# A two-layer block with product-key experts on one core: pacing the gathered tokens through the expert phase

## The chip, the cores and the metric

One core of a Trainium2 chip runs the whole program. The metric is device time in microseconds (us) of one execution.

## The reference

The input x has 256 tokens of 2048 floats. A first block (a norm, a short gated convolution beside block attention, output projection) and the mixing part of a second block (a convolution branch and a state-space branch, gated) come first. The change lies in what follows, the product-key experts:

```python
def peer(h, w_q, sub_keys, u_tab, v_tab):
    def block(xb):                                   # 128 tokens
        q = (xb @ w_q).reshape(128, 8, 2, 128)
        s = jnp.einsum('thcd,hcnd->thcn', q, sub_keys)
        s_top, i_top = lax.top_k(s, 16)              # 16 of 128 keys, twice per head
        cand = s_top[:, :, 0, :, None] + s_top[:, :, 1, None, :]
        cand_idx = i_top[:, :, 0, :, None] * 128 + i_top[:, :, 1, None, :]
        ...
        best, pos = lax.top_k(cand, 16)
        expert = jnp.take_along_axis(cand_idx, pos, axis=-1)
        gates = jax.nn.softmax(best, axis=-1)
        act = jax.nn.gelu(jnp.einsum('td,thkd->thk', xb, u_tab[expert]))
        return jnp.einsum('thk,thkd->td', gates * act, v_tab[expert])
```

Each token picks 8 x 16 = 128 of 16,384 experts; u_tab and v_tab have a row of 2048 floats for each. The result is added to x, and a last norm gives the output. All is float32.

## The kernel before

**Two ways through the experts.** The last 160 tokens (NT) are done densely: both tables, 128 MB each, pass through SBUF in 128 tiles of 1 MB each, every tile is multiplied by all 160 tokens, and a gate matrix that is zero for experts not chosen weighs the activations in between. The first 96 tokens (NS_) are done by gathering: for three groups of 32 tokens the chosen rows are fetched by indirect DMA, 128 rows (1 MB) at a time, four slots of each of 32 tokens. That is 32 gathers of u and 32 of v for a group, 192 in all, called items here.

**The dense stream.** SyncE loads tiles in a fixed order into a ring of five buffers (`w_load`, line 161). `u_step(i)` makes 16 products of u tile i (line 1458), evacuated with a gelu by ScalarE (line 1461); `v_step(i)` makes 16 products of v tile i (line 1475) into sums that stay in PSUM. First come NU0 = 60 u tiles, then v and u tiles in turn for 136 tiles until the u tiles are used up, then v tiles alone. Before v tile i, VectorE multiplies its activations by gates (`weigh`, line 1323), two tiles ahead in program order. The gates come in 16 blocks, built earlier (`gbuild`), stored to DRAM (`gd`) and loaded back eight rows at a time (`gload`, line 1318). The last LAST v tiles are multiplied bank by bank, and each bank is joined with the residual (line 1546), transposed, squared and multiplied by the last gain (lines 1553 to 1556).

**The gathered stream.** `sparse` handles an item as follows. For u, VectorE multiplies the gathered rows by the token's row and sums them (line 1362); after four of them ScalarE makes the gelu (line 1366). For v, after a multiplication by gates (line 1370), VectorE adds the weighted rows to a sum (lines 1372 and 1374). The v items of four slots come after the u items of the next four. There are five buffers; the gather into a buffer (line 1346) is issued by GpSimd when the item that used it is done. After the third group the four partial sums and the residual's rows are loaded (lines 1386, 1387), added (line 1391), normalised and stored (line 1402). `finish(sp_gen)` puts what is left of this in front of the last bank-by-bank part.

**Who decides the order.** All engines execute in program order. Each step of the dense stream calls `Weave.run(budget)`, which draws work from generators until their stated costs (in ns, the numbers they yield) have used the budget; `None` ends a generator's turn. In `gens` are the top-k of the keys (`topk`), then `sparse`, so that `sparse` gets what the top-k leaves; `fine` holds `gbuild`, run four times inside a step. The budget is 3,000 in the query steps, then 4,200 per u tile, or 1,500 while `gbuild` runs (with 675 x 4 for it), then 1,900 per tile. Budgets set an order of instructions only; an engine that waits for nothing runs ahead of the others. `hand_out` gives the first 128 tokens' indices and gates to `rbuf`, from where the gathers read them, once the top-k of these tokens is complete.

When the last u tile is done GpSimd also loads the residual of the dense tokens into the buffers of the normalised input (line 1510 and after).

Of the kernel before, what the change touches and what calls it, by code (L numbers as in the profile page):

```python
# [26 lines left out]
SG = 3  # L27
NS_ = 32 * SG
# [16 lines left out]
class Weave:  # L45
# [34 lines left out]

    def run_fine(self, budget):
# [17 lines left out]
    def finish(self, gen):  # L99
        for _ in gen:  # L100
            pass
        for q in (self.gens, self.free, self.fine):
            if gen in q:
                q.remove(gen)
# [3 lines left out]
def body(ctx, tc, xT, par, wst, kst, bblk, cblk, gfin, uexp, vexp, out):  # L108
# [126 lines left out]

# [874 lines left out]
    gd = drp.tile([NT // 16, P, P, 16], F32, name="gd")  # L1110
    for c in range(2):
        nc.gpsimd.dma_start(xd2[c], x_s[c])
# [87 lines left out]
    sp_ready = [False]  # L1200

    def hand_out():


        V = nc.vector
        V.scalar_tensor_tensor(out=flat(ab[:, 0]), in0=flat(idx[:, 0]), scalar=float(P), in1=flat(idx[:, 1]),
                               op0=ALU.mult, op1=ALU.add)
        V.tensor_copy(flat(abu[:, 0]), flat(ab[:, 0]))
        V.tensor_copy(abr[:, P:2 * P], flat(gat))
        both = abr.rearrange("p (c s) -> p c s", c=2)  # L1210
        for g in range(SG):
            for q in range(4):
                nc.gpsimd.dma_start(
                    rbuf[32 * q:32 * q + 32, 64 * g:64 * g + 64].rearrange("p (c s) -> p c s", c=2),
                    both[32 * g:32 * g + 32, :, 32 * q:32 * q + 32])
        sp_ready[0] = True

    def topk():
        V = nc.vector
        for tt in range(2):  # L1220
# [21 lines left out]
            V.tensor_copy(ixf, ix)  # L1242
            V.tensor_scalar(abu[:, 0], pos, 4, None, op0=ALU.logical_shift_right)
            V.tensor_scalar(abu[:, 1], pos, 15, None, op0=ALU.bitwise_and)
            V.tensor_copy(ab, abu)
# [5 lines left out]
            yield 2500  # L1251
            o4 = scor[tt].rearrange("p (h a b) -> p h a b", h=8, a=16)
            for c in range(2):
                for h in range(0, NH, 4):
                    for q in range(4):
                        V.tensor_tensor(out=o4[:, h + q], in0=ab[:, c, h + q, :, None].to_broadcast([P, 16, 16]),
                                        in1=iota[:, None, 0:16].to_broadcast([P, 16, 16]), op=ALU.is_equal)
                    for q in range(4):
                        V.tensor_tensor(out=o4[:, h + q], in0=o4[:, h + q],
                                        in1=ixf[:, h + q, c, None, :].to_broadcast([P, 16, 16]), op=ALU.mult)  # L1260
                    V.tensor_reduce(out=idx[:, c, h:h + 4, :], in_=o4[:, h:h + 4], axis=AX.X, op=ALU.add)
                    yield 3900
            if tt == 0:
                hand_out()
# [15 lines left out]
    pend_g = []  # L1280

    def gbuild():
        for t4 in range(NT // 4):
            sg = stg[(t4 // 4) % 2].rearrange("p (i t) -> p t i", t=16)
            pb = GB[t4 % 2]
            t = NS_ + t4 * 4
            nc.vector.tensor_tensor(
                out=S[22][:, (t % 8) * P:(t % 8 + 4) * P].rearrange("p (t j) -> p t j", t=4),
                in0=iota[:, None, :].to_broadcast([P, 4, P]),
                in1=i2T[:, t:t + 4, None].to_broadcast([P, 4, P]), op=ALU.is_equal)  # L1290
            for q in range(4):
                o, tq = oh[1][(t + q) % 8], slice(t + q, t + q + 1)
                if q < 1:
                    nc.scalar.activation(o, iota, AF.Abs, scale=-1.0, bias=i1T[:, tq])
                    nc.scalar.activation(o, o, AF.Relu, scale=ngT[:, tq], bias=gT[:, tq])
                else:
                    nc.vector.tensor_scalar(o, iota, i1T[:, tq], gT[:, tq], op0=ALU.is_equal, op1=ALU.mult)
            yield 1650 - 256 * 1
            pend_g.append((t4, pb, sg))
            if len(pend_g) > 1:  # L1300
                gmm(*pend_g.pop(0))
        while pend_g:
            gmm(*pend_g.pop(0))
            yield 500

    def gmm(t4, pb, sg):
# [5 lines left out]
        if t4 % 4 == 3:  # L1312
            nc.scalar.dma_start(gd[t4 // 4], stg[(t4 // 4) % 2].rearrange("p (i t) -> p i t", t=16))

    gblk = lambda b: stg[b % 2][:, 0:8 * NT].rearrange("p (n i t) -> p n i t", n=NT // 16, i=8)

    def gload(b):
        nc.gpsimd.dma_start(gblk(b), gd[:, :, 8 * b:8 * b + 8, :].rearrange("n p i t -> p n i t"))

    def weigh(i):  # L1320

        a3 = act_at(i).rearrange("p (n t) -> p n t", n=NT // 16)
        nc.vector.tensor_tensor(out=a3, in0=a3, in1=gblk(i // 8)[:, :, i % 8, :], op=ALU.mult)  # L1323
        if i % 8 == 7 and i // 8 + 2 < 16:
            gload(i // 8 + 2)


    acc_s, x_rep, gaddr = S[10], S[19], rbuf.bitcast(U32)
    dots = sqsum

    def sparse():
        V = nc.vector
        while not (sp_ready[0] and ws["n"] >= WU):
            yield None
        gb = slots([5, 6, 7, 12, 13])
        flat_b = [(g, n) for g in range(SG) for n in range(8)]
        items = []
        for j, (g, n) in enumerate(flat_b):
            items += [("u", g, 4 * n + k) for k in range(4)]
            if j:  # L1340
                items += [("v", flat_b[j - 1][0], 4 * flat_b[j - 1][1] + k) for k in range(4)]
        items += [("v", SG - 1, 28 + k) for k in range(4)]

        def gather(m):
            kind, g, k = items[m]
            nc.gpsimd.indirect_dma_start(  # L1346
                out=gb[m % len(gb)][:], out_offset=None, in_=uexp if kind == "u" else vexp,
                in_offset=bass.IndirectOffsetOnAxis(ap=gaddr[:, 64 * g + k:64 * g + k + 1], axis=0))

        def rows(g):  # L1350
            for q in range(4):
                nc.gpsimd.dma_start(x_rep[32 * q:32 * q + 32, :], S[18][32 * g:32 * g + 32, :])

        rows(0)
        for m in range(len(gb)):
            gather(m)
        yield None
        for m, (kind, g, k) in enumerate(items):
            buf = gb[m % len(gb)]
            d, a = dots[:, 32 * g + k:32 * g + k + 1], dots[:, P + 32 * g + k:P + 32 * g + k + 1]  # L1360
            if kind == "u":
                V.tensor_tensor_reduce(out=buf, in0=buf, in1=x_rep, scale=1.0, scalar=0.0,  # L1362
                                       op0=ALU.mult, op1=ALU.add, accum_out=d)
# [3 lines left out]
            else:  # L1367
                if k % 4 == 0:
                    a4 = dots[:, P + 32 * g + k:P + 32 * g + k + 4]
                    V.tensor_tensor(out=a4, in0=a4, in1=rbuf[:, 64 * g + 32 + k:64 * g + 36 + k], op=ALU.mult)  # L1370
                if k == 0:
                    V.tensor_scalar(acc_s, buf, a, None, op0=ALU.mult)
                else:
                    V.scalar_tensor_tensor(out=acc_s, in0=buf, scalar=a, in1=acc_s, op0=ALU.mult, op1=ALU.add)  # L1374
            if m + len(gb) < len(items):
                gather(m + len(gb))
            if kind == "u" and k == 31 and g < SG - 1:
                rows(g + 1)
            if kind == "v" and k == 31:
                for q in range(4):  # L1380
                    nc.gpsimd.dma_start(sd[q, 32 * g:32 * g + 32, :], acc_s[32 * q:32 * q + 32, :])
# [39 lines left out]
    weave.add(sp_gen)  # L1421
# [63 lines left out]
    for i in range(NU0):  # L1485
# [13 lines left out]
    LAST = 4  # L1499
    PACE = 1900.0  # L1500
    n_weighed = 0
    for i in range(P - LAST):
# [16 lines left out]
        v_step(i, PACE)  # L1519
        if NU0 + i < P:  # L1520
            u_step(NU0 + i, PACE)
# [124 lines left out]
```

## Time and profile before

| | |
|---|---|
| median of 3 runs | 2566.34 us (2561.63 to 2566.97) |
| the profiled execution | 2564.76 us, its span 2563.0 us |
| TensorE matmuls, weight loads | 2397.4 us (94%), 2270.2 us (89%) |
| VectorE, ScalarE, GpSimd | 1587.9 (62%), 696.5 (27%), 659.5 us (26%) |
| moved by DMA | 741.94 MB, of it 241.81 MB by GpSimd's queue |

Engine names in profile rows: PE is TensorE, PEld its weight loads, DVE VectorE, ACT ScalarE, POOL GpSimd, SP SyncE. L1458 is line 1458 of the kernel. A matmul or weight load appears as two records, so that a tile of 16 products has 32. In square brackets stands the idle time of the engine before the instruction, and what ended it. The span is from the first to the last instruction.

### The profile page before, as it was taken

The numbers are of one execution on the slowest core, as the hardware profiler recorded it, in microseconds if no ns is written. First come the engines' busy times: TensorE is split into PE (matmuls) and PEld (weight loads), VectorE is DVE, ScalarE is ACT, GpSimd is POOL, SyncE is SP. The second block draws the span as 40 slices with busy tenths as digits, with TensorE's granted clock in tenths as the row PEclk, the third lists the DMA queues.
The fourth block names the chain that finished last, engine by engine and source line by source line (L and its number), as shares of the span: only waits on it lengthen the run. The fifth ranks groups of instructions, "written<-read, shape, count | busy, mean of one in ns | idle before, by whom it ended". The sixth has DMA issues, their size and how long they took to land.

```text
span 2563.0 us, 40064 instructions
## 1 busy us (share of the span) xinstructions
PE 2397.4 (94%) x16832; PEld 2270.2 (89%) x16832; DVE 1587.9 (62%) x2379; ACT 696.5 (27%) x1043; POOL 659.5 (26%) x853
## 2 busy tenths in 40 slices
PE   8999999999999999999879994999999899999987
PEld 7888888899999999888879994988888888999887
DVE  6767777589999977567497665344444344414433
ACT  5544454443244445453114520000000000000002
POOL 1887888300000000230202124221111221021100
PEclk9999999999999999999989997999999999999999
DMA  6455556565555444564789999999999999999994
GB/s 234 175 187 188 191 181 215 196 239 206 197 205 183 173 174 176 192 226 165 251 309 389 393 396 360 379 416 421 417 416 416 381 418 416 394 355 412 412 351 176
DMA packets 110004, 741.94 MB, mean 289 GB/s; under 512 B 12832, under 2 KB 13184, under 8 KB 24032
## 3 DMA queue, kind: packets, MB, share of 16 engines
q1 hardware_dynamic: 65760, 474.50, 49.1%
q0 software_dynamic: 36864, 241.81, 23.7%
q10 hardware_dynamic: 7200, 23.07, 2.4%
q8 instruction: 132, 2.16, 0.3%
q14 instruction: 48, 0.39, 0.0%
HBM read 707.00 MB, written 29.10 MB: 287 GB/s over the span
## 4 chain that ended last, share of the span: by engine, by line
PE 63%; DMA 27%; DVE 5%; issue 2%; ACT 1%; POOL 1%; SPq 0%; POOLq 0%; DVEq 0%; ACTq 0%
DMA s<-in_vexp_dram 14%; PE b L270 13%; PE b L1475 10%; PE b L1458 10%; DMA s<-in_wst_dram 9%; PE b L271 7%; PE b L255 4%; PE b L257 4%; PE b L256 4%; PE b L400 2%; DVE s L173 2%; PE b L248 2%; PE b L247 2%; PE b L246 2%; DMA s<-in_uexp_dram,rbuf 2%
## 5 line engine op out<-in xcount | busy, mean ns | idle before, releaser
L1458 PE MATMUL b<-s,s 128*128 128x160 f32 x4096 | 584.9, 302 | 61.3 <-ACT s L1461 38.5
L1475 PE MATMUL b<-s,s 128*128 128x160 f32 x4096 | 583.4, 302 | 54.5 <-DMA s<-in_vexp_dram 44.5
L1458 PEld LDWEIGHTS b<-s,s 128*128 128x128 f32 x4096 | 565.5, 191 | 73.3 <-ACT s L1461 39.2
L1475 PEld LDWEIGHTS b<-s,s 128*128 128x128 f32 x4096 | 563.7, 191 | 71.9 <-issue 57.6
L270 PE MATMUL b<-s,s 128*128 128x512 f32 x1680 | 597.6, 399 | 0.0
L271 PE MATMUL b<-s,s 128*128 128x256 f32 x1680 | 471.5, 281 | 9.1 <-DVE s L173 9.0
L173 DVE TENSOR_TENSOR s<-s,s 128x2048 fp32r<-128x2048 f32 x192 | 452.4, 2358 | 28.1 <-issue 12.3
L1362 DVE CUSTOM_DVE_ANT_0 s<-s,s 128x2048 f32<-128x2048 f32 x96 | 219.7, 2291 | 275.0 <-DMA s<-in_uexp_dram,rbuf 241.6
L270 PEld LDWEIGHTS b<-s,s 128*128 128x128 f32 x1680 | 315.9, 188 | 71.4
L1374 DVE SCALAR_TENSOR_TENSOR s<-s,sqsum,s 128x2048 f32<-128x2048 f32 x93 | 218.7, 2351 | 258.8 <-DMA s<-in_vexp_dram,rbuf 258.1
L167 ACT ACTIVATE s<-s 128x2048 fp32r<-128x2048 f32 x192 | 365.7, 1906 | 9.6 <-DMA s<-in_wst_dram 9.6
L271 PEld LDWEIGHTS b<-s,s 128*128 128x128 f32 x1680 | 317.7, 189 | 13.4 <-DVE s L173 12.6
L255 PE MATMUL b<-s,s 128*128 128x256 f32 x896 | 256.6, 286 | 0.0
L257 PE MATMUL b<-s,s 128*128 128x256 f32 x896 | 253.5, 283 | 0.0
L256 PE MATMUL b<-s,s 128*128 128x256 f32 x896 | 253.5, 283 | 0.0
L1461 ACT ACTIVATE s<-b 128x160 f32<-128x160 f32 x128 | 38.0, 300 | 765.3 <-PE b L1458 756.1
L1346 POOL DMA_INDIRECT s<-in_vexp_dram,rbuf x96 | 106.6, 1110 | 458.8 <-DVE sqsum L1362 196.1
L1346 POOL DMA_INDIRECT s<-in_uexp_dram,rbuf x96 | 114.3, 1191 | 382.3 <-DVE s L1323 174.7
L255 PEld LDWEIGHTS b<-s,s 128*128 128x128 f32 x896 | 171.8, 192 | 3.7 <-issue 2.9
L256 PEld LDWEIGHTS b<-s,s 128*128 128x128 f32 x896 | 171.9, 192 | 0.3
L257 PEld LDWEIGHTS b<-s,s 128*128 128x128 f32 x896 | 171.9, 192 | 0.0
L814 POOL TENSOR_TENSOR sqsum<-sqsum,s 128x256 f32<-128x256 f32 x28 | 57.9, 2067 | 385.5 <-ACT s L812 385.5
(302 smaller groups left out, 2441.8 us busy)
## 6 DMA issues: line engine op xcount, KB each, us to landing
s<-in_wst_dram SPq DMA_DIRECT2D x320, 1024.0 KB
s<-in_vexp_dram SPq DMA_DIRECT2D x128, 1024.0 KB
gd<-s ACTq DMA_DIRECT2D x10, 1024.0 KB
s<-gd POOLq DMA_DIRECT2D x16, 640.0 KB
tabd<-s POOLq DMA_DIRECT2D x32, 256.0 KB
s<-tabd ACTq DMA_DIRECT2D x32, 256.0 KB
xd<-s POOLq DMA_DIRECT2D x4, 1024.0 KB
s<-in_bblk_dram ACTq DMA_DIRECT2D x8, 512.0 KB
```

The lines of the kernel that those rows point to most:

```text
L167: nc.scalar.activation(hi_of(i), raw_of(i), AF.Copy)
L173: nc.vector.tensor_tensor(out=lo_of(i), in0=raw_of(i), in1=FV(hi_of(i)), op=ALU.subtract)
L255: nc.tensor.matmul(ps, a, xh, start=(j == 0), stop=False)
L256: nc.tensor.matmul(ps, a, xl, start=False, stop=False)
L257: nc.tensor.matmul(ps, b, xh, start=False, stop=(j == len(perm) - 1))
L270: nc.tensor.matmul(ps, a, x2, start=(j == 0), stop=False)
L271: nc.tensor.matmul(ps[:, :T], b, x2[:, :T], start=False, stop=(j == len(perm) - 1))
L1346: nc.gpsimd.indirect_dma_start(out=gb[m % len(gb)][:], out_offset=None, in_=uexp if kind == "u" else vexp, in_offset=bass.IndirectOffsetOn ...
L1362: V.tensor_tensor_reduce(out=buf, in0=buf, in1=x_rep, scale=1.0, scalar=0.0, op0=ALU.mult, op1=ALU.add, accum_out=d)
L1374: V.scalar_tensor_tensor(out=acc_s, in0=buf, scalar=a, in1=acc_s, op0=ALU.mult, op1=ALU.add)
L1458: nc.tensor.matmul(ps, raw[:, k * P:(k + 1) * P], nv(k)[:, NS_:T], start=(k == 0), stop=(k == KT - 1))
L1475: nc.tensor.matmul(acc[d], raw[:, d * P:(d + 1) * P], act_at(i), start=False, stop=(i == P - 1 and (d % 3 == 2 or d == KT - 1)))
```

## The change

- `sparse` leaves `gens`. It is drawn by a new `run_paced`, once per step, at 0.78 items per tile (0.78 x 2350), from the moment it is started.
- `hand_out` is split: the indices go first, and with them the first gathers are issued at once (`sp_start`); the gates follow after the softmax. The picks of the first four heads (turning positions into indices) are made inside the top-k, after head 5.
- Four turns (AHEAD) pass before the first item; a gelu is emitted two items after its last u item.
- Budgets: 2,600 for the top-k and 4 x 650 for `gbuild` through all 60 u tiles, 0 afterwards.
- The first two gate blocks are loaded from ScalarE's queue.
- LAST is 2 in place of 4.
- Groups of 32 tokens are written as a list, and gate blocks for a count of tokens that 16 does not divide are added; with 160 dense tokens the added parts stay empty.

```diff
+        self.paced = []
+        self.pace, self.paced_credit = 0.78 * 2350, 0
...
+    def run_paced(self):
+        for gen in list(self.paced):
+            self.paced_credit = min(self.paced_credit + self.pace, self.pace)
+            while self.paced_credit > 0:
+                try:
+                    cost = next(gen)
...
+                if cost is None:
+                    break
+                self.paced_credit -= cost
...
         weave.run(budget)
+        weave.run_paced()
...
-    def hand_out():
+    def hand_out(c):
...
+        for g, (t0, n) in enumerate(GROUPS):
             for q in range(4):
-                nc.gpsimd.dma_start(
-                    rbuf[32 * q:32 * q + 32, 64 * g:64 * g + 64].rearrange("p (c s) -> p c s", c=2),
-                    both[32 * g:32 * g + 32, :, 32 * q:32 * q + 32])
-        sp_ready[0] = True
+                nc.gpsimd.dma_start(rbuf[n * q:n * q + n, 64 * g + 32 * c:64 * g + 32 * c + 32],
+                                    abr[t0:t0 + n, P * c + 32 * q:P * c + 32 * q + 32])
+        if c == 0:
+            sp_start()
...
+                if h == 5:
+                    yield from picks(tt, 0)
+            yield from picks(tt, 4)
+            if tt == 0:
+                hand_out(0)
             V.tensor_tensor(out=gat, in0=best, in1=best[:, :, 0:1].to_broadcast([P, 8, 16]), op=ALU.subtract)
             nc.scalar.activation(gat, gat, AF.Exp)
+            yield 1500
...
             if tt == 0:
-                hand_out()
+                hand_out(1)
...
-    def gload(b):
-        nc.gpsimd.dma_start(gblk(b), gd[:, :, 8 * b:8 * b + 8, :].rearrange("n p i t -> p n i t"))
+    def gload(b, eng):
+        eng.dma_start(gblk(b), gd[:, :, 8 * b:8 * b + 8, :].rearrange("n p i t -> p n i t"))
...
+    def sp_start():
...
+        gb.extend(slots([5, 6, 7, 12, 13]))
+        for m in range(len(gb)):
+            gather(m)
+            if m == 0:
+                rows(0)
+        weave.paced.append(sp_gen)
...
     def sparse():
         V = nc.vector
-        while not (sp_ready[0] and ws["n"] >= WU):
+        for _ in range(AHEAD):
             yield None
...
                 if k % 4 == 3:
-                    lo, hi = 32 * g + k - 3, 32 * g + k + 1
-                    nc.scalar.activation(dots[:, P + lo:P + hi], dots[:, lo:hi], AF.Gelu_apprx_tanh)
+                    late.append((m + 2, acts[:, k - 3:k + 1], dots_[:, k - 3:k + 1]))
...
+            while late and m >= late[0][0]:
+                _, dst, src = late.pop(0)
+                nc.scalar.activation(dst, src, AF.Gelu_apprx_tanh)
...
-    weave.add(sp_gen)
...
-        u_step(i, 1500.0 if weave.fine else 4200.0, 2700.0 / 4)
+        u_step(i, 2600.0, 2600.0 / 4)
     for g in (sc_gen, tk_gen, gb_gen):
         weave.finish(g)
-    gload(0)
-    gload(1)
+    gload(0, nc.scalar)
+    gload(1, nc.scalar)
...
-    LAST = 4
-    PACE = 1900.0
+    LAST = 2
...
-        v_step(i, PACE)
+        v_step(i, 0.0)
         if NU0 + i < P:
-            u_step(NU0 + i, PACE)
+            u_step(NU0 + i, 0.0)
```

## Rows read from the trace of the kernel before

**Rows 1.** The page, part 2: the span in 40 slices.

```profile
DMA  6455556565555444564789999999999999999994
GB/s 234 175 187 188 191 181 215 196 239 206 197 205 183 173 174 176 192 226 165 251 309 389 393 396 360 379 416 421 417 416 416 381 418 416 394 355 412 412 351 176
```

**Rows 2.** The chain that ended last: start us, us, work.

```profile
2260.72 73.91 PE b L1475 x544
```

**Rows 3.** Windows: us, busy PE, PEld, DVE, ACT, POOL; clock, DMA, GB/s.

```profile
1660.00:2225.00 565.00, 515.66 (x3615) 493.85 (x3616) 246.83 (x229) 18.01 (x67) 112.88 (x115) 1.00 1.01 412
...
2336.00:2460.00 124.00, 115.36 (x811) 110.58 (x810) 57.61 (x61) 1.90 (x4) 19.43 (x20) 1.00 1.01 411
2470.00:2500.00 30.00, 23.96 (x161) 23.32 (x160) 7.57 (x6) 0.00 (x0) 1.00 (x2) 0.94 1.02 277
```

**Rows 4.** Timeline of TensorE, v and u tiles: start us, us, work, idle.

```profile
2195.90 4.58 PE L1475 MATMUL b<-s,s 128*128 128x160 f32 x32 [0.38 <-DMA s<-in_vexp_dram]
2200.86 4.59 PE L1458 MATMUL b<-s,s 128*128 128x160 f32 x32 [0.38 <-DMA s<-in_wst_dram]
```

**Rows 5.** Timeline of VectorE in the same stretch.

```profile
2207.48 2.29 DVE L1362 CUSTOM_DVE_ANT_0 s<-s,s 128x2048 f32<-128x2048 f32 x1 [2.30 <-DMA s<-in_uexp_dram,rbuf]
...
2212.45 2.29 DVE L1362 CUSTOM_DVE_ANT_0 s<-s,s 128x2048 f32<-128x2048 f32 x1 [2.44 <-DMA s<-in_uexp_dram,rbuf]
```

**Rows 6.** Timeline of TensorE, first 60 tiles and first v tile.

```profile
1295.21 15.00 PE L1458 MATMUL b<-s,s 128*128 128x160 f32 x95 [20.34 <-ACT s L1461]
...
1519.78 23.68 PE L1458 MATMUL b<-s,s 128*128 128x160 f32 x160 [3.85 <-ACT s L1461]
1557.73 10.94 PE L1458 MATMUL b<-s,s 128*128 128x160 f32 x64 [14.27 <-ACT s L1461]
...
1590.55 7.24 PE L1475 MATMUL b<-s,s 128*128 128x160 f32 x32 [9.97 <-DVE s L1323]
```

**Rows 7.** Timeline of ScalarE, the first gelu of the gathered tokens.

```profile
1294.76 0.20 ACT L1366 ACTIVATE sqsum<-sqsum 128x4 f32<-128x4 f32 x1 [27.76 <-DVE sqsum L1362]
```

**Rows 8.** Timeline of VectorE, two heads of the top-k.

```profile
1301.50 0.41 DVE L1232 TENSOR_TENSOR s<-s 128x256 f32<-128x256 f32 x1
...
1306.00 0.41 DVE L1232 TENSOR_TENSOR s<-s 128x256 f32<-128x256 f32 x1
```

**Rows 9.** Timeline of GpSimd: gathers, gate blocks, residual, row reload.

```profile
1268.66 1.04 POOL L1346 DMA_INDIRECT s<-in_uexp_dram,rbuf  x1 [0.30 <-issue]
...
1575.42 2.08 POOL L1318 DMA_DIRECT2D s<-gd  x2
...
2258.84 0.94 POOL L1510 DMA_DIRECT2D s<-xd  x1 [52.69 <-PE b L1458]
...
2268.99 0.95 POOL L1346 DMA_INDIRECT s<-in_uexp_dram,rbuf  x1 [0.30 <-issue]
...
2429.88 0.94 POOL L1346 DMA_INDIRECT s<-in_vexp_dram,rbuf  x1 [4.02 <-DVE s L1323]
...
2471.23 0.51 POOL L1387 DMA_DIRECT2D s<-xrow  x1
```

**Rows 10.** Windows of the gathers: us, busy (count), clock, DMA, GB/s.

```profile
1225.00:1590.00 365.00, 68.21 (x51) 0.92 0.91 357
1590.00:2262.00 672.00, 122.78 (x110) 1.00 0.99 398
```

**Rows 11.** Timeline of VectorE at the end.

```profile
2457.37 2.35 DVE L1374 SCALAR_TENSOR_TENSOR s<-s,sqsum,s 128x2048 f32<-128x2048 f32 x1 [2.50 <-DMA s<-in_vexp_dram,rbuf]
...
2508.84 0.55 DVE L1323 TENSOR_TENSOR s<-s,s 128x160 f32<-128x160 f32 x2
2532.11 0.66 DVE L1546 TENSOR_TENSOR s<-b,s 128x480 f32<-128x480 f32 x1 [22.72 <-PE b L1475]
...
2549.14 0.64 DVE L1546 TENSOR_TENSOR s<-b,s 128x480 f32<-128x480 f32 x1
...
2552.10 0.30 DVE L1546 TENSOR_TENSOR s<-b,s 128x160 f32<-128x160 f32 x1
```

More of the change, by code (lines that the diff above doesn't have):

```diff
@@ L26 @@
 NEG = -1e30
-SG = 3
-NS_ = 32 * SG
+GROUPS = [(0, 32), (32, 32), (64, 32)]
+NS_ = 96
 NT = T - NS_
@@ L79, in run @@
                 self.credit -= cost
+    def run_paced(self):
[4 more added lines that the diff above has]
+                    cost = next(gen)
+                except StopIteration:
+                    self.paced.remove(gen)
+                    break
+                if cost is None:
+                    break
+                self.paced_credit -= cost
     def run_fine(self, budget):
@@ L101, in finish @@
             pass
-        for q in (self.gens, self.free, self.fine):
+        for q in (self.gens, self.free, self.fine, self.paced):
             if gen in q:
@@ L1110, in body @@
     gd = drp.tile([NT // 16, P, P, 16], F32, name="gd")
+    GT, GR = NT // 16 * 16, NT % 16
     for c in range(2):
@@ L1199, in body @@
     flat = lambda ap: ap.rearrange("p h k -> p (h k)")
-    sp_ready = [False]
-    def hand_out():
+    def hand_out(c):
         V = nc.vector
[L1206 to L1211, printed above, removed]
-            for q in range(4):
-                nc.gpsimd.dma_start(
-                    rbuf[32 * q:32 * q + 32, 64 * g:64 * g + 64].rearrange("p (c s) -> p c s", c=2),
-                    both[32 * g:32 * g + 32, :, 32 * q:32 * q + 32])
-        sp_ready[0] = True
+        if c == 0:
+            V.scalar_tensor_tensor(out=flat(ab[:, 0]), in0=flat(idx[:, 0]), scalar=float(P), in1=flat(idx[:, 1]),
+                                   op0=ALU.mult, op1=ALU.add)
+            V.tensor_copy(flat(abu[:, 0]), flat(ab[:, 0]))
+        else:
+            V.tensor_copy(abr[:, P:2 * P], flat(gat))
+        for g, (t0, n) in enumerate(GROUPS):
+            for q in range(4):
+                nc.gpsimd.dma_start(rbuf[n * q:n * q + n, 64 * g + 32 * c:64 * g + 32 * c + 32],
+                                    abr[t0:t0 + n, P * c + 32 * q:P * c + 32 * q + 32])
+        if c == 0:
+            sp_start()
@@ new lines, in picks @@
+    def picks(tt, h):
+        V = nc.vector
+        hs = slice(h, h + 4)
+        V.tensor_copy(ixf[:, hs], ix[:, hs])
+        V.tensor_scalar(abu[:, 0, hs], pos[:, hs], 4, None, op0=ALU.logical_shift_right)
+        V.tensor_scalar(abu[:, 1, hs], pos[:, hs], 15, None, op0=ALU.bitwise_and)
+        V.tensor_copy(ab[:, :, hs], abu[:, :, hs])
+        yield 900
+        o4 = scor[tt].rearrange("p (h a b) -> p h a b", h=8, a=16)
+        for c in range(2):
+            for q in range(4):
+                V.tensor_tensor(out=o4[:, h + q], in0=ab[:, c, h + q, :, None].to_broadcast([P, 16, 16]),
+                                in1=iota[:, None, 0:16].to_broadcast([P, 16, 16]), op=ALU.is_equal)
+            for q in range(4):
+                V.tensor_tensor(out=o4[:, h + q], in0=o4[:, h + q],
+                                in1=ixf[:, h + q, c, None, :].to_broadcast([P, 16, 16]), op=ALU.mult)
+            V.tensor_reduce(out=idx[:, c, hs, :], in_=o4[:, hs], axis=AX.X, op=ALU.add)
+            yield 3900
@@ L1250, in topk @@
             V.tensor_tensor(out=gat, in0=gat, in1=gsum[:, 8:16, None].to_broadcast([P, 8, 16]), op=ALU.mult)
[L1251 to L1262, printed above, removed]
             if tt == 0:
-                hand_out()
+                hand_out(1)
             yield None
@@ L1280, in body @@
     pend_g = []
+    rest = S[24][:, 0:P * GR].rearrange("p (i t) -> p i t", t=GR) if GR else None
     def gbuild():
         for t4 in range(NT // 4):
-            sg = stg[(t4 // 4) % 2].rearrange("p (i t) -> p t i", t=16)
+            sg = stg[(t4 // 4) % 2].rearrange("p (i t) -> p t i", t=16) if t4 * 4 < GT else rest.rearrange("p i t -> p t i")
             pb = GB[t4 % 2]
@@ L1311, in gmm @@
                              pb.rearrange("p (t i) -> p t i", t=4), AF.Copy)
-        if t4 % 4 == 3:
+        if t4 % 4 == 3 and t4 * 4 < GT:
             nc.scalar.dma_start(gd[t4 // 4], stg[(t4 // 4) % 2].rearrange("p (i t) -> p i t", t=16))
-    gblk = lambda b: stg[b % 2][:, 0:8 * NT].rearrange("p (n i t) -> p n i t", n=NT // 16, i=8)
-    def gload(b):
-        nc.gpsimd.dma_start(gblk(b), gd[:, :, 8 * b:8 * b + 8, :].rearrange("n p i t -> p n i t"))
+    gblk = lambda b: stg[b % 2][:, 0:8 * GT].rearrange("p (n i t) -> p n i t", n=GT // 16, i=8)
@@ L1320, in weigh @@
+    def gload(b, eng):
+        eng.dma_start(gblk(b), gd[:, :, 8 * b:8 * b + 8, :].rearrange("n p i t -> p n i t"))
     def weigh(i):
-        a3 = act_at(i).rearrange("p (n t) -> p n t", n=NT // 16)
+        a = act_at(i)
+        a3 = a[:, 0:GT].rearrange("p (n t) -> p n t", n=GT // 16)
         nc.vector.tensor_tensor(out=a3, in0=a3, in1=gblk(i // 8)[:, :, i % 8, :], op=ALU.mult)
+        if GR:
+            nc.vector.tensor_tensor(out=a[:, GT:NT], in0=a[:, GT:NT], in1=rest[:, i, :], op=ALU.mult)
@@ L1324, in weigh, with gather @@
         if i % 8 == 7 and i // 8 + 2 < 16:
-            gload(i // 8 + 2)
+            gload(i // 8 + 2, nc.gpsimd)
     acc_s, x_rep, gaddr = S[10], S[19], rbuf.bitcast(U32)
+    AHEAD = 4
     dots = sqsum
+    items = []
+    for j in range(8 * len(GROUPS) + 1):
+        for kind, n in (("u", j), ("v", j - 1)):
+            if 0 <= n < 8 * len(GROUPS):
+                items += [(kind, n // 8, n % 8 * 4 + k) for k in range(4)]
+    gb = []
+    def gather(m):
+        kind, g, k = items[m]
+        n = 4 * GROUPS[g][1]
+        nc.gpsimd.indirect_dma_start(
+            out=gb[m % len(gb)][0:n, :], out_offset=None, in_=uexp if kind == "u" else vexp,
+            in_offset=bass.IndirectOffsetOnAxis(ap=gaddr[0:n, 64 * g + k:64 * g + k + 1], axis=0))
@@ L1331, in sparse, with rows @@
+    def rows(g):
+        t0, n = GROUPS[g]
+        for q in range(4):
+            nc.gpsimd.dma_start(x_rep[n * q:n * q + n, :], S[18][t0:t0 + n, :])
+    def sp_start():
+        assert ws["n"] >= WU and len(q_ready) == KT and s_ready[0] == NH
+        gb.extend(slots([5, 6, 7, 12, 13]))
[4 more added lines that the diff above has]
+        weave.paced.append(sp_gen)
     def sparse():
         V = nc.vector
-        while not (sp_ready[0] and ws["n"] >= WU):
+        for _ in range(AHEAD):
@@ L1334, in sparse @@
             yield None
[L1335 to L1357, printed above, removed]
+        late = []
         for m, (kind, g, k) in enumerate(items):
-            buf = gb[m % len(gb)]
-            d, a = dots[:, 32 * g + k:32 * g + k + 1], dots[:, P + 32 * g + k:P + 32 * g + k + 1]
+            t0, n = GROUPS[g]
+            buf = gb[m % len(gb)][0:4 * n, :]
+            dots_, acts = dots[0:4 * n, 32 * g:32 * g + 32], dots[0:4 * n, P + 32 * g:P + 32 * g + 32]
+            ac = acc_s[0:4 * n, :]
@@ L1361, in sparse @@
             if kind == "u":
-                V.tensor_tensor_reduce(out=buf, in0=buf, in1=x_rep, scale=1.0, scalar=0.0,
-                                       op0=ALU.mult, op1=ALU.add, accum_out=d)
+                V.tensor_tensor_reduce(out=buf, in0=buf, in1=x_rep[0:4 * n, :], scale=1.0, scalar=0.0,
+                                       op0=ALU.mult, op1=ALU.add, accum_out=dots_[:, k:k + 1])
                 if k % 4 == 3:
-                    lo, hi = 32 * g + k - 3, 32 * g + k + 1
-                    nc.scalar.activation(dots[:, P + lo:P + hi], dots[:, lo:hi], AF.Gelu_apprx_tanh)
+                    late.append((m + 2, acts[:, k - 3:k + 1], dots_[:, k - 3:k + 1]))
@@ L1367, in sparse @@
             else:
+                a = acts[:, k:k + 1]
                 if k % 4 == 0:
-                    a4 = dots[:, P + 32 * g + k:P + 32 * g + k + 4]
-                    V.tensor_tensor(out=a4, in0=a4, in1=rbuf[:, 64 * g + 32 + k:64 * g + 36 + k], op=ALU.mult)
+                    a4 = acts[:, k:k + 4]
+                    V.tensor_tensor(out=a4, in0=a4, in1=rbuf[0:4 * n, 64 * g + 32 + k:64 * g + 36 + k], op=ALU.mult)
                 if k == 0:
-                    V.tensor_scalar(acc_s, buf, a, None, op0=ALU.mult)
+                    V.tensor_scalar(ac, buf, a, None, op0=ALU.mult)
@@ L1373, in sparse @@
                 else:
-                    V.scalar_tensor_tensor(out=acc_s, in0=buf, scalar=a, in1=acc_s, op0=ALU.mult, op1=ALU.add)
+                    V.scalar_tensor_tensor(out=ac, in0=buf, scalar=a, in1=ac, op0=ALU.mult, op1=ALU.add)
+            while late and m >= late[0][0]:
+                _, dst, src = late.pop(0)
+                nc.scalar.activation(dst, src, AF.Gelu_apprx_tanh)
             if m + len(gb) < len(items):
                 gather(m + len(gb))
-            if kind == "u" and k == 31 and g < SG - 1:
+            if kind == "u" and k == 31 and g < len(GROUPS) - 1:
```

6 lines of the change are left out of this document (1 added, 5 removed).

## Prediction

> **What bounds the kernel now.** I read the page's slices first, because they separate two kinds of kernel. Up to the middle of the span the DMA engines are half busy; from the 22nd slice on, the expert phase, they stand at nine tenths or more [rows 1]. So there the question is not only "is TensorE busy" but "what else is on the channel". The expert phase passes 256 tiles of 1 MB through a ring of five buffers: 60 first-table (u) tiles alone, then 136 passes that alternate second (v) and first table, then 60 v tiles. Beside them run 192 gathers of 1 MB, whose products VectorE makes. When everything has arrived a tile costs TensorE 4.35 us: 17 tiles (544 records of 32) in 73.91 us [rows 2].
>
> Then the windows by stretch [rows 3]. From 1660 to 2225 TensorE is busy 515.7 of 565 us while the DMA share is 1.01 at 412 GB/s: the channel sets the pace. There a tile starts every 4.96 us [rows 4], and gathered products also follow each other by 4.97 us [rows 5]: tiles and gathers take turns, one each. Last, the timeline of TensorE before that stretch [rows 6] has three waits for a ScalarE evacuation of the u tiles, 20.34, 3.85 and 14.27 us. ScalarE was not busy: it stood 27.76 us in front of the gathered tokens' gelu, which waits for VectorE's dot products [rows 7], and those wait for gathers. A later wait, 9.97 us for L1323, is for the gate blocks.
>
> **The change, part by part, as a row of milestones.** The sum is made against the profiled span, 2563.0 us, whose execution took 2564.76 us; that is 1.6 us under the median of 2566.34.
>
> *First 60 tiles.* Before, gathered items shared one budget with the top-k and took what was left of 4,200 per tile once the gate building was over: 1.8 items per tile, more than the channel gives; TensorE then paid through ScalarE. After, an item is handed out 0.78 times per tile everywhere. When? Heads six and seven and the last merge cost 3 x 4,000 in the generator's figures and the second half of the picks 8,700; at 2,600 per tile, and starting at tile 2 where the last scores are there, that is tile 10. The gathers are issued there and used from tile 14; the first gelu is emitted with the sixth item, near tile 20, some 45 us after the issue. Before, the first gelu ran at 1294.76, 26 us after the first issue at 1268.66 [rows 7, 9], and TensorE had already waited 20 us for it. So I take all three waits away: 38.5 us, and the u tiles end at 1557.73 + 10.94 - 38.5 = 1530 us. Against this, top-k at 2,600 really costs 2.93 us (a head priced 4,000 takes 1306.00 - 1301.50 = 4.50 us [rows 8]), plus 1.8 for 0.78 items: 4.7 us of VectorE in a 4.35 us tile, for 22 tiles 8 us of delay, which the distance of 45 us covers. Without that cover it is 8 us on the path. The lower TensorE clock that such waits leave (a tile of 7.24 us at 1590.55 [rows 6]), a gain, I set against a fuller channel, a loss.
> The second half of top-k, 54,900 at 2,600, ends near tile 36, the gate building, 40 x 1,394 at 2,600, near tile 58: still inside the 60. Splitting the hand-out gives GpSimd twelve more small DMAs (each some 0.51 us, like the small one at 2471.23 [rows 9]), 6 us behind the first five gathers, where GpSimd would wait for a free buffer anyway; costed at nothing, else 6 us.
>
> *First v tile.* The gate blocks are now loaded from ScalarE's queue, no longer behind gathers on GpSimd's. But the last store of the gates is issued only at tile 58, and ScalarE stands in front of the load until it has landed, with the evacuation of tile 60 behind it. Before, TensorE lost 1590.6 - 1568.7 = 21.9 us there (a few of them with opening the sums); the loads alone took from 1575.4 to the start at 1590.5 [rows 6, 9]. Bounds: 11 us (15.1 less one tile) and 22 us; I take 17, as nothing shortens the landing itself. First v tile at 1547 us, 43 earlier.
>
> *136 alternating tiles.* Before: 1590.6 to 2262, 671 us, with 110 gathers [rows 10]. The slower hand-out does not slow the engines: GpSimd and VectorE run ahead of TensorE until a gelu holds them, so only the count matters. Items at tile 196: 0.78 x 182 = 142 (before: 51 + 110 gathers less five ahead, 156); with the buffers ahead 148 gathers issued against 161. At tile 60 it is 42 against 51. So 106 gathers fall into this stretch, four fewer: 4 x 2.55 us (1.05 MB at 412 GB/s) = 10 us. The moved gelu lets VectorE lead by two items less, which changes no count. At its end GpSimd still stands in front of the reload of the residual until the last u tile is done, 52.69 us before [rows 9], with the gathers behind it. End at 1547 + 661 = 2208 us.
>
> *Last 60 tiles.* Here the price comes. 44 gathers are left instead of 31. Before, five were issued at once and the other 26 every (2429.88 - 2268.99) / 26 = 6.19 us [rows 9], gate blocks between them, and the last product ended 198 us after the start of the stretch [rows 11]. 13 more are 80 us. TensorE needs 17 tiles at 4.35 and 43 at 4.9 (811 records in 124 us [rows 3]), 285 us, and its last loads have landed by then, so the last four gathers run alone at 1.05 MB / 421 GB/s (the fuller slices [rows 1]) = 2.5 us: 15 us back. Last product at 2208 + 198 + 65 = 2471 us. Summing, normalising and storing those tokens kept VectorE until 2508.8, 49 us [rows 11], of which some 30 were the reading back of 4 MB, while the channel moved 277 GB/s and half of that was tiles [rows 3]. Alone that is 14 us, hence 33. Bounds 33 and 49; I take 40: VectorE free at 2511 us. TensorE is through its tiles at 2208 + 285 = 2493, so the gathered tokens now end last, by 18 us.
>
> *End.* From the first join to the end of the span it was 30.9 us, with (2549.14 - 2532.11) / 4 = 4.3 us per bank of four tiles. With two tiles the chain of transpose, square, product and join binds, 2.96 us as between the last two joins [rows 11]: 5 us less. The two tiles that go back into the loop cost 8.7 us only if TensorE ends last. 26 us, and the span is 2537; with the 1.8 and 1.6 us the median is **2540 us**.
>
> The Trainium skill ("DMA: Bandwidth & Descriptors", Queues, rings and completion order) says that every DMA engine goes round robin over the queues that have work. The equal turns of 4.96 and 4.97 us agree; by that rule a lower rate of hand-out frees no bandwidth while gathers are outstanding, and the sum would stay as it is, or be the third case below where the first 60 tiles have to share as well.
>
> **Rivals.**
> *The channel is used without dips.* Groups of 32 tokens change twice in the alternating stretch and its mean is 412, not 421 GB/s. With no loss, 251 MB-sized transfers at 2.49 us and some 15 us for the blocked queue are 640 us, and with gathers every 4.97 us the last stretch is bound by TensorE: 1547 + 640 + 285 + 26 = 2498, median 2501. For it: the free-running gathers at 4.97. Against: the same group changes remain. Chance 0.22.
> *The first 60 tiles become channel bound.* Gathers run from tile 14 on; where tiles share equally they take 4.96 us, 0.61 more, over the 23 tiles before gate building 14 us, and with the gate wait at 22 us the whole shifts by 19: 2559. Against: the ring hid that for 17 tiles after 2262. Chance 0.12.
> *Slower: the gathered tail runs away.* In the last stretch alone the gathers set the end, so each 0.1 us of their spacing costs 4.4 us over 44. From 6.9 us each, where it was 6.19, the time passes 2571. At 7.2 us it is 2584. For it: GpSimd's queue carries the gate blocks and the residual's reload between them. Against: the mean of 6.19 already holds these. Chance 0.13.
>
> **How the numbers follow.** The forecast, 2515 to 2560 us, has 0.53. A measurement of this kernel tells about 0.2% from no change, 2561.2 to 2571.5. Faster: 0.53 + 0.22 = 0.75; within 0.2%: 0.12; slower: 0.13. The range, 2502 to 2576, takes in the half of the first rival that ends above 2501 and a third of the last: 0.53 + 0.11 + 0.12 + 0.04 = 0.8.
>
> **What would show it.** Right: no wait of TensorE for L1461's line over 5 us among the u tiles; first v tile near 1547; some 40 to 46 gathers after the last u tile; joins that wait for VectorE's sums of the gathered tokens, not for TensorE. Wrong: a ScalarE wait in front of a gelu that is still 15 us or more; tiles at 4.96 us before the gate building; a last gathered product before 2440 or after 2500.

## The result, and the profile after

The changed kernel takes 2533.39 us (median of 4, 2531.59 to 2536.68) against 2566.65 us: a ratio of 0.9872, 95% interval 0.9851 to 0.9894. The profiled execution took 2536.68 us, its span is 2534.9 us. The predicted median was 2540, the predicted span 2537.

The page, part 2, to be read against [rows 1]:

```profile
span 2534.9 us, 40085 instructions
...
DMA  6455546566555444555699998999999999999995
GB/s 236 169 197 184 185 180 216 195 229 216 198 210 180 173 180 168 186 210 194 224 391 420 400 386 349 416 388 417 416 416 416 397 388 411 364 411 411 413 420 147
```

The slices of the expert phase are filled earlier (391 GB/s in the 21st, 309 before) and the dip in the middle of it is shorter: one slice under 380 GB/s (349), where [rows 1] have two (360 and 379). Next the milestones. First GpSimd's and ScalarE's timelines around the first 60 tiles (L1373 is the gather, L1230 the hand-out, L1417 the gathered tokens' gelu, L1341 the store of the gates, L1346 their load):

```profile
1251.31 3.94 POOL L1230 DMA_DIRECT2D rbuf<-s  x8 [115.03 <-DVE s L1284]
...
1258.58 1.04 POOL L1373 DMA_INDIRECT s<-in_uexp_dram,rbuf  x1 [0.30 <-issue]
...
1271.53 0.56 POOL L1230 DMA_DIRECT2D rbuf<-s  x1 [2.42 <-DVE s L1211]
...
1283.02 0.50 POOL L1230 DMA_DIRECT2D rbuf<-s  x1 [5.00 <-DMA s<-in_uexp_dram,rbuf]
...
1298.49 1.57 POOL L1230 DMA_DIRECT2D rbuf<-s  x3 [0.17 <-issue]
```

```profile
1312.18 0.30 ACT L1503 ACTIVATE s<-b 128x160 f32<-128x160 f32 x1 [4.04 <-PE b L1500]
1312.38 0.20 ACT L1417 ACTIVATE sqsum<-sqsum 128x4 f32<-128x4 f32 x1
```

```profile
1527.15 0.33 ACTq L1341 DMA_DIRECT2D gd<-s  x1
1528.19 0.30 ACT L1503 ACTIVATE s<-b 128x160 f32<-128x160 f32 x1 [1.07 <-PE b L1500]
1539.38 3.61 ACTq L1346 DMA_DIRECT2D s<-gd  x2
```

The first gather goes out at 1258.58, 10 us earlier than in [rows 9]. The first gelu runs at 1312.38 without idle time in front of it, where [rows 7] had 27.76 us. ScalarE issues the load of the gates only at 1539.38, 12 us after the last store. TensorE at the first v tile:

```profile
1548.74 6.85 PE L1517 MATMUL b<-s,s 128*128 128x160 f32 x32 [15.09 <-DVE s L1352]
```

It is the only idle time over 0.5 us that TensorE has between 1225 and 1550; the three waits of [rows 6] for ScalarE are gone. The u tiles end at 1532.5. Then the gathers by stretch, cut at the first v tile and at the last u tile (columns as in [rows 10], the count in parentheses), and GpSimd in front of the residual's reload (L1551):

```profile
1225.00:1548.70 323.70, 52.21 (x42) 0.98 0.96 377
1548.70:2206.00 657.30, 137.48 (x106) 0.99 0.99 400
2206.00:2535.00 329.00, 42.66 (x44) 0.95 0.91 360
```

```profile
2204.10 0.94 POOL L1551 DMA_DIRECT2D s<-xd  x1 [47.51 <-PE b L1500]
```

The counts are 42, 106 and 44, where [rows 10] had 51 and 110 and left 31. Last, the end: VectorE's last two gathered products (L1414), the sums of the gathered tokens (L1434), the first and the last join (L1587), and TensorE's first transpose:

```profile
2468.84 2.35 DVE L1414 SCALAR_TENSOR_TENSOR s<-s,sqsum,s 128x2048 f32<-128x2048 f32 x1 [2.62 <-DMA s<-in_vexp_dram,rbuf]
2473.83 2.35 DVE L1414 SCALAR_TENSOR_TENSOR s<-s,sqsum,s 128x2048 f32<-128x2048 f32 x1 [2.63 <-DMA s<-in_vexp_dram,rbuf]
2491.32 2.29 DVE L1434 TENSOR_TENSOR s<-s,s 96x2048 f32<-96x2048 f32 x1 [15.14 <-DMA s<-sd]
...
2500.74 2.29 DVE L1434 TENSOR_TENSOR s<-s,s 96x2048 f32<-96x2048 f32 x1 [0.27 <-DMA s<-xrow]
...
2508.55 0.65 DVE L1587 TENSOR_TENSOR s<-b,s 128x480 f32<-128x480 f32 x1
...
2524.28 0.30 DVE L1587 TENSOR_TENSOR s<-b,s 128x160 f32<-128x160 f32 x1
```

```profile
2466.94 16.92 PE L1517 MATMUL b<-s,s 128*128 128x160 f32 x120 [0.38 <-DMA s<-in_vexp_dram]
2509.26 1.54 PE L1594 MATMUL b<-ident,s 128*128 128x128 f32 x6 [25.40 <-DVE s L1587]
```

At 2483.9 TensorE has done all that it can before the first join (of the last two tiles, the first two of six banks) and waits 25.40 us for that join, which stands behind the sums of the gathered tokens in VectorE's order. In [rows 11] it was the other way round: VectorE waited 22.72 us for TensorE.

### The profile page after: what moved, and what is told of

It is laid out like the page before. It is cut to its first block, busy times and chain, and to the rows that moved or that the text cites. A ratio compares the mean times of both kernels' runs of the same rounds, so it can differ in the third digit from the quotient of the medians.

```text
span 2534.9 us, 40085 instructions
## 1 busy us (share of the span) xinstructions
PE 2394.7 (94%) x16832; PEld 2267.7 (89%) x16832; DVE 1587.2 (63%) x2387; ACT 699.4 (28%) x1045; POOL 677.4 (27%) x863
## 4 chain that ended last, share of the span: by engine, by line
PE 64%; DMA 28%; DVE 5%; ACT 1%; issue 1%; POOL 0%; SPq 0%; DVEq 0%; ACTq 0%; POOLq 0%
PE b L287 14%; PE b L1500 14%; DMA s<-in_wst_dram 9%; DMA s<-in_vexp_dram 8%; PE b L288 7%; DMA s<-in_vexp_dram,rbuf 6%; PE b L1517 5%; PE b L272 4%; PE b L274 4%; PE b L273 4%; DMA s<-in_uexp_dram,rbuf 3%; PE b L417 2%; PE b L265 2%; PE b L264 2%; PE b L263 2%; DVE s L189 1%
## 5 line engine op out<-in xcount | busy, mean ns | idle before, releaser
L1414 DVE SCALAR_TENSOR_TENSOR s<-s,sqsum,s 128x2048 f32<-128x2048 f32 x93 | 218.6, 2350 | 159.3 <-DMA s<-in_vexp_dram,rbuf 158.7
L1373 POOL DMA_INDIRECT s<-in_uexp_dram,rbuf x96 | 124.5, 1297 | 395.8 <-DVE s L1352 212.7
L1373 POOL DMA_INDIRECT s<-in_vexp_dram,rbuf x96 | 107.8, 1123 | 446.5 <-DVE s L1352 244.4
```

Of the source, the lines that this page charges most:

```text
L1373: nc.gpsimd.indirect_dma_start(out=gb[m % len(gb)][0:n, :], out_offset=None, in_=uexp if kind == "u" else vexp, in_offset=bass.IndirectOff ...
L1414: V.scalar_tensor_tensor(out=ac, in0=buf, scalar=a, in1=ac, op0=ALU.mult, op1=ALU.add)
```

## The experiments

All changes are to the changed kernel unless another is named. It was run again as a control.

> The changed kernel once more, unaltered, beside the next three: 2531 to 2537 us.

Measured: 2533.66 us (2529.89 to 2536.07), ratio to the kernel before 0.9865 (0.9850 to 0.9880). The three runs beside it were those with 0.74 and 0.86 items per tile and the last one below, with 0.72.

### Is it the even rate or the later gelu that removed the waits?

```diff
-                    late.append((m + 2, acts[:, k - 3:k + 1], dots_[:, k - 3:k + 1]))
+                    late.append((m, acts[:, k - 3:k + 1], dots_[:, k - 3:k + 1]))
```

> The changed kernel (2533 us) with the gelu back right behind its fourth u item. Theory (the even rate of hand-out removed the waits of TensorE for ScalarE; the distance of four turns covers the first gathers): no such wait over 3 us among the u tiles, 2528 to 2538 us. Rival (the later gelu is what removed them): waits of 10 to 20 us are back, 2545 to 2570 us.

Measured: 2545.17 us, 0.9915 (0.9901 to 0.9928). Neither: the time lies at the lower edge of the rival's range, but no wait of TensorE for ScalarE over 0.4 us came back and the first v tile stands at 1547.75. Against the control 12 us are lost in the median, and 8.1 us in the spans of the two profiled executions (2543.0 for 2534.9). These 8 us are lost by the last u tile, which is done at 2214.0 instead of 2206.0. GpSimd's row there, and the windows of the gathers just before it, first with the gelu at once, then the changed kernel:

```profile
2212.16 0.94 POOL L1551 DMA_DIRECT2D s<-xd  x1 [70.47 <-PE b L1500]
```

```profile
2060.00:2200.00 140.00, 23.81 (x15) 1.00 0.94 380
```

```profile
2060.00:2200.00 140.00, 24.86 (x15) 1.00 0.97 393
```

These rows are read so: the earlier gelu lets VectorE and GpSimd run further ahead of TensorE. GpSimd then stands longer in front of the residual's reload, 70.47 for 47.51 us, sends no gathers in that time, and the channel moves 380 for 393 GB/s. As many gathers are left (44), and the last u tile is 8 us later. The later gelu is thus worth some 8 to 12 us, not as a remedy for waits but as a shorter leash.

```diff
-    AHEAD = 4
+    AHEAD = 0
```

together with the gelu at once:

> The changed kernel with no turns before the first item and the gelu right behind its fourth u item. Theory: the early issue and the top-k between the items leave the first gelu at tile 14, near 1290 us, about when the fourth product is there; a wait of 0 to 8 us, and three items more are handed out by the last u tile; 2522 to 2540 us. Rival (the distance alone covers the first gathers): the wait of 20 us at the first gelu is back, 2545 to 2560 us.

Measured: 2540.88 us, 0.9894 (0.9878 to 0.9909), 1 us above the theory's range. TensorE's timeline:

```profile
1297.01 23.67 PE L1500 MATMUL b<-s,s 128*128 128x160 f32 x160 [5.35 <-ACT s L1503]
1322.83 65.47 PE L1500 MATMUL b<-s,s 128*128 128x160 f32 x480 [2.15 <-ACT s L1503]
```

5.35 and 2.15 us, not 20: early issue and even hand-out together cover most of the first gathers without the four turns; how much each of them does is not separated. As the theory had it, three gathers fewer are left at the last u tile (41 for 44), and TensorE's wait at the first join is 13.67 us, where it was 25.25 in the run before. The time is 4 us less than there, with intervals that just overlap.

The other way round, the kernel before without its burst of items:

```diff
-        u_step(i, 1500.0 if weave.fine else 4200.0, 2700.0 / 4)
+        u_step(i, 1500.0 if weave.fine else 4200.0 if tk_gen in weave.gens else 1900.0, 2700.0 / 4)
```

> The kernel before with 1,900 in place of 4,200 per u tile once the top-k is through, so without the burst of items before tile 60; nothing else. Theory: the two waits of 3.9 and 14.3 us go, but some 11 gathers move behind the last u tile, where they set the end: 2552 to 2570 us against 2566. Rival (the waits are pure loss): 18 us faster, 2544 to 2550 us.

Measured: 2565.42 us, 0.9987 (0.9978 to 0.9996). Of the three waits for ScalarE of [rows 6] only the first is left:

```profile
1296.92 64.03 PE L1458 MATMUL b<-s,s 128*128 128x160 f32 x448 [20.44 <-ACT s L1461]
...
1566.12 6.07 PE L1475 MATMUL b<-s,s 128*128 128x160 f32 x32 [15.82 <-DVE s L1323]
```

```profile
1225.00:1566.00 341.00, 55.30 (x40) 0.95 0.91 350
1566.00:2236.00 670.00, 122.81 (x110) 0.99 0.99 399
2236.00:2563.00 327.00, 40.53 (x42) 0.94 0.90 356
```

The first v tile is 24 us earlier, and the time is only 2 to 3 us less than that of the kernel before beside it (2565.42 for 2567.76). The last u tile is done at 2232.1; with the one gather that goes out between it and the cut at 2236, 43 gathers are left for 31, and now TensorE waits for the gathered tokens (23.9 us in three waits of its transposes, L1553, for VectorE's joins, L1546). Waits that were removed early came back at the end. This is the clearest of the runs.

### Does it matter who loads the first gate blocks?

```diff
-    gload(0, nc.scalar)
-    gload(1, nc.scalar)
+    gload(0, nc.gpsimd)
+    gload(1, nc.gpsimd)
```

> The changed kernel with the first two gate blocks loaded from GpSimd's queue again. Theory: the landing of the last gate store (12 us) sets the first v tile, whoever issues the load; GpSimd is done with its gathers by 1530; no change, 2530 to 2537 us. Rival (standing behind gathers on GpSimd's queue was the cost): the first v tile 5 to 10 us later, 2538 to 2545 us.

Measured: 2534.01 us, 0.9874 (0.9859 to 0.9889): no change. TensorE's waits:

```profile
1538.15 2.50 PE L1513 MATMUL b<-s 128*128 128x480 f32 x6 [7.87 <-POOL s L1510]
1544.41 7.44 PE L1517 MATMUL b<-s,s 128*128 128x160 f32 x32 [3.76 <-DVE s L1352]
```

The load now holds up GpSimd's memset (L1510), which opens the sums, but the first v tile stands at 1544.41, no later than in the control (1546.04). GpSimd issues the load at 1535.52, 11 us after the last store (1524.93); ScalarE did it 12 us after. So the queue is not what counts. That both wait for the landing of the store is the likely reason, but the profile names another transfer at GpSimd's wait, so it is not shown.

### Which side ends last?

```diff
-    LAST = 2
+    LAST = 4
```

> The changed kernel (2533 us) with four tiles per bank at the end again. Theory (the gathered tokens end last, TensorE stands 25 us in front of the first join): the two tiles are not hidden any more but done between the joins, so 4.3 instead of 3.0 us per bank, 5 us slower, 2535 to 2542 us. Rival (TensorE's tiles set the end): two tiles leave the path, 4 us faster, 2527 to 2531 us.

Measured: 2540.55 us, 0.9902 (0.9884 to 0.9920): 7 us slower than the control. TensorE at the first transpose:

```profile
2508.60 1.54 PE L1594 MATMUL b<-ident,s 128*128 128x128 f32 x6 [22.78 <-DVE s L1587]
```

It still waits 22.78 us there, and the two tiles that could be done in that wait now lie behind it: from the first join to the last it takes 20.3 us, where the changed kernel takes 15.7.

Three other rates, here the first; the others replace the same number:

```diff
-        self.pace, self.paced_credit = 0.78 * 2350, 0
+        self.pace, self.paced_credit = 0.82 * 2350, 0
```

> The changed kernel with 0.82 items per tile for 0.78. Theory (gathers left after the last u tile set the end): 0.04 x 182 = 7 fewer are left, 37 for 44; each costs 2.6 us before the last u tile and saves 5 to 6 us after it, until TensorE ends last; 2518 to 2528 us. Rival (the lower rate relieves the channel, so a higher one costs): 2538 to 2550 us.

> The changed kernel with 0.74 items per tile. Theory (gathers left after the last u tile set the end): some 51 are left for 44, the gathered tokens end 25 us later relative to a last u tile that is 18 us earlier or less, so 2540 to 2562 us. Rival (a lower rate relieves the channel and TensorE): 2515 to 2530 us.

> The changed kernel with 0.86 items per tile. At 0.82 TensorE and the gathered tokens ended within 2 us of each other. Theory: from there on TensorE ends last, and seven gathers more before the last u tile delay it by 2.6 us each; some 29 gathers left; 2530 to 2545 us. Rival (fewer gathers left is always better): under 2524 us.

| items per tile | gathers left at the last u tile | first join | median, us | ratio to before |
|---|---|---|---|---|
| 0.74 | 51 | 2515.9 | 2547.63 | 0.9920 (0.9907 to 0.9934) |
| 0.78 (control) | 44 | 2505.4 | 2533.66 | 0.9865 (0.9850 to 0.9880) |
| 0.82 | 36 | 2498.2 | 2526.94 | 0.9847 (0.9833 to 0.9860) |
| 0.86 | 29 | 2501.7 | 2529.78 | 0.9848 (0.9834 to 0.9861) |

TensorE at 0.74, then VectorE at 0.86, at the first join:

```profile
2516.63 1.54 PE L1594 MATMUL b<-ident,s 128*128 128x128 f32 x6 [42.12 <-DVE s L1587]
```

```profile
2501.73 0.66 DVE L1587 TENSOR_TENSOR s<-b,s 128x480 f32<-128x480 f32 x1 [30.56 <-PE b L1517]
```

At 0.74 TensorE waits 42.12 us for VectorE, at 0.86 VectorE 30.56 us for TensorE, and at 0.82 neither waits more than 0.5 us for the other at the first join. The rate moves work between two ends that both have to finish, and 0.82 is near the point where they meet. It is faster than the kernel before, and 0.2 to 0.3% faster than the changed one; that last difference is small, and the intervals of the two ratios overlap. 0.86 came out just under the range expected, and at 0.86 and 0.82 the intervals coincide, so no optimum between them is claimed.

### Is GpSimd's wait for the last u tile a loss?

```diff
-            nc.gpsimd.dma_start(xq[0][:, 0:8 * NT].rearrange("p (d t) -> p d t", d=8),
+            nc.scalar.dma_start(xq[0][:, 0:8 * NT].rearrange("p (d t) -> p d t", d=8),
...
-            nc.gpsimd.dma_start(xq[0][:, 8 * NT:9 * NT], xd2[1][:, NS_:T])
-            nc.gpsimd.dma_start(xq[1][:, 0:7 * NT].rearrange("p (d t) -> p d t", d=7),
+            nc.scalar.dma_start(xq[0][:, 8 * NT:9 * NT], xd2[1][:, NS_:T])
+            nc.scalar.dma_start(xq[1][:, 0:7 * NT].rearrange("p (d t) -> p d t", d=7),
```

> The changed kernel with the three reloads of the residual issued by ScalarE, so that GpSimd's gathers don't stand 47 us behind the last u tile. Theory (the blocked queue leaves the channel idle, 260 of 421 GB/s for 47 us): some 5 to 8 gathers come before the last u tile, 36 to 39 are left, 2515 to 2528 us. Rival (VectorE is held there by the gelu anyway, and the gathers with it): no change, 2530 to 2537 us.

> Both: 0.82 items per tile and the residual's reload by ScalarE. Theory: the gathered tokens end with the tiles or before them, and TensorE sets the end; 2510 to 2522 us, little under either alone. Rival (the channel is full either way): as 0.82 alone, within 3 us.

> The residual's reload by ScalarE with 0.72 items per tile. With 0.78 it left 36 gathers for 44, but TensorE then ended last, after two losses of the channel to gathers behind the last u tile. Theory (only the balance counts, the channel's work is the same): the lower rate gives the tiles back what they lost, 2520 to 2534 us. Rival (the gathers that no longer stand there cost the tiles more than they bring): 2536 us or more.

Measured: 2540.99 us (0.9902, 0.9886 to 0.9917) at 0.78, 2548.91 us (0.9928, 0.9913 to 0.9943) at 0.82, 2534.71 us (0.9872, 0.9856 to 0.9889) at 0.72. At 0.78 the theory had the count right and the time wrong; at 0.78 and at 0.82 the run was slower than theory and rival allowed, and at 0.72 it lies between the two. One caution: the profiled execution at 0.78 was the fastest of four, 2533.54 us, which is the time of the changed kernel; the other three took 2540.80 to 2542.76 us and left no trace. Its rows can show why nothing was gained, not where the 7 us of the median went. Gathers, TensorE and the first join at 0.78:

```profile
1541.00:2200.00 659.00, 148.94 (x114) 0.99 1.00 405
2200.00:2531.00 331.00, 38.35 (x36) 0.95 0.90 347
```

```profile
2279.16 24.93 PE L1517 MATMUL b<-s,s 128*128 128x160 f32 x160 [15.71 <-DMA s<-in_vexp_dram]
...
2458.12 48.64 PE L1517 MATMUL b<-s,s 128*128 128x160 f32 x344 [3.52 <-DMA s<-in_vexp_dram]
```

```profile
2505.16 0.66 DVE L1587 TENSOR_TENSOR s<-b,s 128x480 f32<-128x480 f32 x1 [33.64 <-PE b L1517]
```

36 gathers are left for 44 and the last product is at 2418, 58 us earlier. But the gathers had run on at the tiles' cost: TensorE waits 15.71 us for a tile at 2279, ends last, and VectorE waits 33.64 us for it. The windows behind the last u tile (columns as in [rows 3]), first the changed kernel, then this run:

```profile
2206.00:2281.00 75.00, 75.00 (x553) 74.92 (x553) 23.82 (x27) 0.60 (x3) 18.25 (x19) 1.00 1.00 402
```

```profile
2200.00:2280.00 80.00, 56.06 (x389) 53.33 (x388) 42.20 (x48) 0.81 (x4) 21.16 (x18) 0.92 1.02 405
```

After the pause TensorE ran 75 of 75 us; here it is busy 56.06 of 80, with the same traffic. Nor was the channel idle in the changed kernel's pause: it moved 419 GB/s or more until 2180, 390 for the next 10 us and only then 260, the figure that the theory had for all 47, where a tile every 4.35 us takes 241 (an estimate: 1.05 MB in 4.35 us). So the tiles came in faster than TensorE used them until, most likely, the ring was full; its filling was not measured apart. At 0.82 it is worse (VectorE waits 67.73 us), at 0.72 the balance is back (TensorE waits 1.98 us at the first transpose) and the time is that of the changed kernel. So GpSimd's pause of 47 us was not a loss that can be had back by issuing more gathers.

## Why the prediction was right

| milestone | before | predicted | measured |
|---|---|---|---|
| end of the first 60 tiles | 1568.7 | 1530 | 1532.5 |
| first v tile | 1590.6 | 1547 | 1548.7 |
| gathers in the three stretches | 51, 110, 31 | 42, 106, 44 | 42, 106, 44 |
| last u tile | 2260.7 (taken as 2262) | 2208 | 2206 |
| last gathered product | 2459.7 | 2471 | 2476.2 |
| VectorE free for the joins | 2508.8 | 2511 | 2508.5 |
| end of the span | 2563.0 | 2537 | 2534.9 |

Read the last two rows together. VectorE is free at the same time as before, but before, the first join waited for TensorE until 2532.1; now TensorE comes first and the join starts when VectorE is free. That is 23.6 of the 28.1 us that the span lost; the rest came after the first join.

*First 60 tiles.* Right, waits and size. The run without the burst shows that handing out fewer items there removes the second and third wait. For the first wait, early issue and distance count: with the gelu at once and four turns no wait is left, without the turns 5.35 and 2.15 us, 7.5 us in all, close to the 8 that the prediction gave for the case without cover. The split hand-out, the earlier picks and the new budgets were not taken back one by one, so what each of them does for the first wait stays open. One sign of being wrong did show up in part: nine tiles before the gate building start some 4.97 us apart, among them these, at a cost of 5 to 6 us by the prediction's 0.61 a tile.

```profile
1371.07 4.59 PE L1500 MATMUL b<-s,s 128*128 128x160 f32 x32 [0.39 <-ACT s L1503]
1376.04 4.58 PE L1500 MATMUL b<-s,s 128*128 128x160 f32 x32 [0.38 <-ACT s L1503]
```

*The split hand-out* was priced at 6 us, 0.51 us for each of twelve DMAs, and costed at nothing, because GpSimd would wait for a free buffer anyway. Both reasons failed. It held GpSimd's queue from 1271.53 to 1300.6, 29 us: four of the twelve were issued after waits of 4.3 to 5.0 us, which the profile puts down to gathers' landings. And the buffer was free long before, after VectorE's first product:

```profile
1277.27 2.29 DVE L1402 CUSTOM_DVE_ANT_0 s<-s,s 128x2048 f32<-128x2048 f32 x1 [0.82 <-DMA s<-s]
```

The sixth gather went out only at 1301.62, 22 us after that product. TensorE paid nothing for it, as the first gelu came without a wait: the nothing came out right, but not for the reason given.

*First v tile.* Right: 16.2 us for 17. The prediction named the move to ScalarE's queue but gave its 17 us to the landing of the store; with the load back on GpSimd the queue is shown to make no difference.

*Alternating tiles.* 657 us for 661, with exactly the 106 gathers forecast. One sentence failed: "The moved gelu lets VectorE lead by two items less, which changes no count." The count is unchanged, but the inference that the edit is worth nothing here was wrong; undoing it costs 12 us in the median, 8 of them before the last u tile.

*Last 60 tiles.* The count is right, two terms are not. The last four gathers were to run alone, 2.5 us each, for 15 us back; the last products still stand 4.97 to 4.99 us apart, and tiles were still being loaded until shortly before, so that term did not come. Against it, the first gather went out 2 us after the last u tile (2208.13) where before it was 8, and from the issue of the last gather to the end of its product it took 24.6 us for 29.8. The spacing, taken as the prediction took it, was 6.24 us for 6.19. Together that makes 270 us to the last product for 263. Then the sums took 32.3 us for the 40 taken, just under the lower bound of 33: TensorE's last wait for a tile ended at 2466.94, before the rows were stored (from 2476.47) and read back, and VectorE waited 15.14 us for the first of them, where the kernel before waited 22.57. That the errors of +7 and -8 us cancel is luck. TensorE was forecast through all its tiles at 2493; at 2483.9 it lacks 20 products, some 5 us of work (an estimate: 16 take 4.35 us). That the gathered tokens end last is shown by the wait of 25.40 us, by LAST, and by the three rates.

*End.* 26.4 us for 26, and the joins 3.1 us apart for 2.96; the run with LAST at 4 confirms the term, 4.6 us for 5.

Of the 6.6 us between 2540 and 2533.4 two are in the span. The rest is the step from one execution to the median, which is chance: the profiled execution was taken to lie 1.6 us under its median as before, and lay 3.3 us above it.

The rivals fell: the channel did have its dips (407 to 412 GB/s between 1660 and 2060, 400 over the alternating tiles), tiles did slow before the gate building, but nine of them and not 23, and the tail did not run away: its gathers stand 6.24 us apart, not 6.9 or more. What bears the third rival out in part is that the end is set by the gathered tokens, as the rates show.

## What to carry to other kernels

Where two streams share one channel and both must finish, count what each has left at the point where they stop hindering each other; a wait removed early is paid back at the end unless that balance is moved too, as the run without the burst shows (the 3.85 and 14.27 us of [rows 6] gone, 2 to 3 us gained). A rate written into program order does not limit engines that run ahead, but it fixes how much is issued in front of the next wait that all of them share. So sweep it after every other edit: 0.04 items per tile was worth 7 us (0.78 to 0.82) and 14 us (0.74 to 0.78) here, LAST 7 us and the later gelu 12.

## What was not expected of the hardware

- A queue that stands idle can be worth something: behind 47 us without new gathers TensorE ran 75 us without a wait, and without that pause the kernel took 7 us more in the median at the same rate.
- Small DMAs of 0.5 us behind large gathers in GpSimd's queue: four of twelve were issued about 5 us apart, each after a wait that the profile puts down to a gather's landing.
